# Pacing partition moves, reordering the first slab of two matmul groups, and giving the last sigmoids their own buffer

## The chip, the cores and the metric

The kernel runs on one core of a Trainium2 chip. The metric is the device time of one execution in microseconds (us). The kernel before takes 1146.32 us (median of 3 runs, 1145.93 to 1146.48). Engines: PE is TensorE, ACT is ScalarE, DVE is VectorE, SP issues most DMAs.

## The reference, cut to what matters

One decoder layer on 256 tokens with 2048 channels, all in float32. Only the last parts are touched:

```
y = rms(h);  h = h + (silu(y @ w_gate) * (y @ w_up)) @ w_down      # D_FF = 5632 = 11 * 512
y = rms(h);  h = h + sigmoid(y @ w_ple_gate) * (p @ w_ple_proj)
out = rms(h) * final_norm_g
```

Before them stand an input projection, four mixers and an output projection.

## The kernel before, in words

**Layout.** The residual is held channel-major: 16 tiles of 128 channels (partitions) by 256 tokens. Every float32 operand of a product is split into a high part that TensorE reads in its fast 32-bit format (F32R) and a low part (the rest); a product is high x high, high x low and low x high.

**Slabs.** Weights stream in slabs of 512 rows by 512 columns (1 MB). `load_slab` (L236) issues the DMA into one of 3 `raw` buffers; ACT then writes `whi` (a copy, 128x2048) and DVE writes `wlo` = raw - whi. There are 3 `whi` and 3 `wlo` buffers, so the split of a slab waits until PE has finished the slab three before it. `run` (L411) keeps two slabs loaded ahead of the one that is multiplied; after each slab's matmuls it calls `pump(budget)` (L300), which runs deferred work by cost until a credit is used up. The order in which the code emits work is close to the order on each engine, but the framework may put a ready instruction ahead of one that still waits. Each engine runs its own list in order.

**The gated feed-forward part.** `ffn` (L789) is called four times, with 3, 3, 3 and 2 column groups of 512 (`FFN_CUTS`, L29): the gate and the up product of each group, and then four `w_down` groups over all that the call has made. A group is 4 slabs (16 for the whole of D). There are two forms:

- all groups of a call but the last (7 in all) are token-major (`group_t`, L772): the activations are the stationary operand and the result is 128 tokens by 512 channels, in one PSUM bank for each half of the tokens. `ev_gate_t` and `ev_up_t` finish them; the product must then be turned to channel-major. DVE transposes it in blocks of 32x32 into a tile `turned`, and `move` (L838) carries the blocks to their partitions: 4 ACT copies of 32 partitions by 256 for each quarter i of each half t, so 8 moves and 32 copies a group. They are deferred at a cost of 1.0 each, with a budget of 2.0 a slab (`BUDGET_FFN`) and an overdraft of 2.0: 4 moves behind the group's last slab, 2 behind each of the next two.
- the last group of a call (4 in all) is channel-major (`group`, L326, `wide_out`): 4 outputs m of 128 channels, each in a PSUM bank of its own, [whi x hi + ..., wlo x hi] side by side. `ev_gate` and `ev_up` read each bank twice, ACT first and DVE after it, and no turning is needed. The first slab goes through all four outputs with whi and then through all four with wlo.

There are 6 PSUM banks for all of these products, in rotation. A channel-major group takes 4, so outputs 2 and 3 of the up group write the banks from which outputs 0 and 1 of the gate group before it are read out.

**The end.** The last 512 columns of `w_ple_gate` are done token-major: token half 0 in `last_a` (L1010), half 1 in `last_b` (L1023) in two column halves q. `gate_last` (L971) makes z = sigmoid(bank) on ACT, multiplies and adds on DVE, sums squares on ACT; `finish` (L987) makes the reciprocal root, scales, stores, and returns `rest`, which multiplies the other 12 channel tiles by a row of PSUM (5 DVE operations `h<-h,ps_bc`) and stores them. The z of half t lies in `g_row[1 + t]`.

**The pool `asp`.** It has 7 buffers (tag "a") of 8 KB a partition. At the end it holds 4 tiles of the normed residual, 2 tiles `kept` with the split of the last product's first slab (read by both token halves) and the row tile `g_row`. `load_g` (L921) evaluates `asp.tile(...)` inside a generator, so that it asks for four tiles, not for four parts of one.

Of the kernel before, what the change touches and what calls it, by code (L numbers as in the profile page):

```python
# [9 lines left out]
F32 = mybir.dt.float32  # L10
# [5 lines left out]
P = 128  # L16
# [3 lines left out]
KD = D // P  # L20
GW = 512
# [10 lines left out]
CONV_DVE = 8  # L32
BUDGET = 2.8
BUDGET_OUT = 2.8
BUDGET_FFN = 2.0
OVERDRAFT = 2.0
WARM = 9

# [14 lines left out]
def trunk(ctx: ExitStack, tc: tile.TileContext, xT, pT, par, w_in, sgu_wT, sgu_lb, sgu_b,  # L53
# [5 lines left out]
    asp = ctx.enter_context(tc.tile_pool(name="asp", bufs=7))  # L59
# [7 lines left out]
    def act(out, in_, func=AF.Copy, bias=0.0, scale=1.0):  # L67
        nc.scalar.activation(out, in_, func, bias=bias, scale=scale)  # L68

    def tt(out, a, b, op):  # L70
        nc.vector.tensor_tensor(out=out, in0=a, in1=b, op=op)  # L71
# [7 lines left out]
    def short():  # L79
        return work.tile([P, T], F32, tag="short", name="short", bufs=9)  # L80

    def duo(pad=PADP):

        return work.tile([P, 2, PADP + T], F32, tag="duo", name="duo", bufs=5)[:, :, PADP - pad:]
# [12 lines left out]
    def bank():  # L97
        return mm.tile([P, 512], F32, tag="mm", name="ps_mm")

    def wk(tag, n=T, bufs=2):  # L100
        return work.tile([P, n], F32, tag=tag, name=tag, bufs=bufs)
# [130 lines left out]
    steps = []  # L232
    now, credit = [0], [0]
    bg, fill = [], deque()
# [61 lines left out]
    def defer(cost, fn, wait=0):  # L296

        bg.append((now[0] + wait, cost, fn))

    def pump(n):  # L300

        credit[0] += n
        while credit[0] > -OVERDRAFT:
            i = next((i for i, x in enumerate(bg) if x[0] <= now[0]), None)
            if i is not None:
                _, cost, fn = bg.pop(i)
            elif fill and credit[0] > 0:
                cost, fn = fill.popleft()
            else:
                credit[0] = min(credit[0], 0.0)  # L310
                return
            fn()
            credit[0] -= cost
# [5 lines left out]
    def flush():  # L319

        while bg or fill:
            now[0] += 0 if any(x[0] <= now[0] for x in bg) else 1
            pump(1e9)
        credit[0] = 0
# [77 lines left out]
    def token_products(ps, t, tiles, parts, start, stop, x=slice(0, 512)):  # L402

        c = slice(t * P, (t + 1) * P)
        for j, (a, (whi, wlo)) in enumerate(zip(tiles, parts)):
            nc.tensor.matmul(ps, a[:, 0, c], whi[:, x], start=start and j == 0, stop=False)  # L406
            nc.tensor.matmul(ps, a[:, 0, c], wlo[:, x], start=False, stop=False)  # L407
            nc.tensor.matmul(ps, a[:, 1, c], whi[:, x], start=False,  # L408
                             stop=stop and j == len(tiles) - 1)
# [13 lines left out]
    full = [(i, 4) for i in range(0, KD, 4)]  # L423
# [284 lines left out]
    def project(cols, evac, **kw):  # L708
# [4 lines left out]
            hooks={1: [stats_first], 2: [rest_first]})  # L713
# [55 lines left out]
    hs2, h2_parts = [None] * KD, Quads()  # L769
    acc3 = wk("acc", bufs=2)  # L770

    def group_t(w, g, evac, hooks=None):  # L772

        ps = []

        def body(i, parts):
            if i == 0:
                ps.extend(bank() for _ in range(TT))
            for t in range(TT):
                token_products(ps[t], t, hs[4 * i:4 * i + 4], parts, i == 0, i == 3)  # L780
                if i == 3:
                    evac(t, ps[t])
            for f in (hooks or {}).get(i, ()):
                f()

        for i in range(KD // 4):
            steps.append(((w, 4 * i, 4, [(g * GW, GW)]), lambda p, i=i: body(i, p), BUDGET_FFN))

    def ffn(g0, ng, final):  # L789
        acts = Quads()  # L790
        gs = {}

        def ev_gate(m, ps):
            l = short()
            act(l, ps[:, T:])
            z = short()
            tt(z, ps[:, :T], l, ALU.add)
            tt(z, z, stats["ffn"][1], ALU.mult)
            s = short()
            act(s, z, AF.Sigmoid)  # L800
            tt(s, s, stats["ffn"][1], ALU.mult)
            gs[m] = short()
            tt(gs[m], z, s, ALU.mult)

        def ev_up(m, ps):
            l = short()
            act(l, ps[:, T:])
            o = short()
            tt(o, ps[:, :T], l, ALU.add)
            tt(o, o, gs[m], ALU.mult)  # L810
            split(o, acts[4 * (ng - 1) + m])

        def ev_gate_t(t, ps):
            r = stats["ffn"][0][:, t:t + 1]
            s = wide()
            act(s, ps, AF.Sigmoid, scale=r)
            gs[t] = wide()
            stt(gs[t], ps, r, s, ALU.mult, ALU.mult)  # L820

        def ev_up_t(n):
            turned = []

            def f(t, ps):
                if not turned:
                    turned.append(asp.tile([P, TT, 2, GW], F32, tag="a", name="turned"))
                o, hi = gs[t], wide()
                stt(o, ps, stats["ffn"][0][:, t:t + 1], o, ALU.mult, ALU.mult)
                act(hi.bitcast(F32R), o)  # L830
                tt(o, o, hi, ALU.subtract)
                nc.vector.transpose(out=turned[0][:, t, 0, :], in_=hi)
                nc.vector.transpose(out=turned[0][:, t, 1, :], in_=o)
                for i in range(4):
                    defer(1.0, lambda i=i: move(n, t, i, turned[0]))
            return f

        def move(n, t, i, turned):  # L838
            acts[4 * n]
            c = slice(t * P + 32 * i, t * P + 32 * i + 32)  # L840
            for j in range(4):
                act(acts.q[n][32 * j:32 * j + 32, :, :, c].rearrange("p m s b -> p s m b"),
                    turned[32 * i:32 * i + 32, t].rearrange(
                        "p s (m j b) -> p s m j b", m=4, j=4)[:, :, :, j, :])

        def hidden(i):
            if bg:
                flush()
            return [acts[k] for k in range(4 * i, 4 * i + 4)]

        h4s = lambda i: hs[4 * i:4 * i + 4]
        for n, g in enumerate(range(g0, g0 + ng)):
            hooks = ({i + 1: [f] for i, f in enumerate(stats_hooks(acc2, "ffn"))}
                     if g == 0 else None)
            if n < ng - 1:
                group_t(w_gate, g, ev_gate_t, hooks)
                group_t(w_up, g, ev_up_t(n))
            else:
                group(w_gate, [(g * GW, GW)], full, h4s, ev_gate, BUDGET_FFN, wide_out=True)
                group(w_up, [(g * GW, GW)], full, h4s, ev_up, BUDGET_FFN, wide_out=True)  # L860
        for g in range(4):
            def ev(m, ps, g=g):
                j = 4 * g + m
                add_residual(j, ps)
                if final:
                    hs2[j] = split(h[j], h2_parts[j], col("g_ple", j))
                    square(j, acc3)
            group(w_down, [(g * GW, GW)], [(4 * g0 + k, 4) for k in range(0, 4 * ng, 4)],
                  hidden, ev, wide_out=True,
                  hooks={0: [(lambda: load_p()) if g == 2 else (lambda: p_tiles(0))]}  # L870
                  if final and g > 1 else None)
# [40 lines left out]
    for g in range(3):  # L912
        group(w_pp, [(g * GW, GW)], [(0, 2)], p_tiles, evac_p(g),
              hooks={0: [ple_stats[0]]} if g == 2 else None)
# [4 lines left out]
    h_last, base, g_row = [None] * TT, [], []  # L919

    def load_g():  # L921
        g_row.extend(asp.tile([P, 4, GW], F32, tag="a", name="g_row")[:, i] for i in range(4))
        nc.sync.dma_start(out=g_row[0], in_=g_last.broadcast_to([P, GW]))

    def turn(t):
# [22 lines left out]
    for g in range(3):  # L948
        def ev(m, ps, g=g):
# [7 lines left out]
            if m == 3:  # L957
                gated()

        hooks = {0: [ple_stats[1], load_g], 1: [lambda: turn(0)], 2: [lambda: turn(1)]}  # L960
        group(w_pg, [(g * GW, GW)], full, lambda i: hs2[4 * i:4 * i + 4], ev, wide_out=True,
              hooks=hooks if g == 0 else None)
# [6 lines left out]
    z_last, zg_last, part = [None] * TT, [None] * TT, [None] * TT  # L969

    def gate_last(t, q, ps):  # L971

        if q == 0:
            z_last[t] = g_row[1 + t].rearrange("p (a t) -> p a t", a=2)
            zg_last[t] = wide()
            part[t] = wk("part", 2)
        z, x = z_last[t][:, q, :], slice(q * T, (q + 1) * T)
        act(z, ps, AF.Sigmoid, scale=stats["ple"][0][:, t:t + 1])
        tt(z, z, pp_last[t][:, x], ALU.mult)
        tt(z, z, h_last[t][:, x], ALU.add)  # L980
        nc.scalar.activation(short(), z, AF.Square, scale=D ** -0.5,
                             accum_out=part[t][:, q:q + 1])
        tt(zg_last[t][:, x], z, g_row[0][:, x], ALU.mult)
        if q == 0:
            ts(part[t][:, 0:1], part[t][:, 0:1], base[0][:, t:t + 1], ALU.add, -0.5, ALU.mult)
# [97 lines left out]
```

## Time and profile before

| what | value |
|---|---|
| median of the runs | 1146.32 us |
| the profiled execution | 1146.52 us |
| its span, first to last instruction | 1144.8 us |
| PE / PEld / DVE / ACT busy | 98 / 85 / 67 / 57 % |
| chain that ended last | PE 85 %, ACT 6 %, DVE 5 %, issue 3 %, DMA 1 % |
| mean share of the 16 DMA engines in use by the weight queue | 55.3 % |
| granted TensorE clock, mean | 0.996 |

In a timeline a row is a run of equal instructions: start, time from the first start to the last end, engine, line, operation, what it writes and reads, count, and in brackets the idle time of the engine before it with what ended it. Matmuls are pipelined: one lasts longer in the rows than the step from its start to the next.

### The profile page before, as it was taken

To read this page: it belongs to the slowest core of one execution; us is meant where nothing else is said; L and a number is where in the kernel's file an instruction comes from. 1 tells how busy PE (TensorE), PEld (TensorE's weight loads), DVE (VectorE), ACT (ScalarE), POOL (GpSimd) and SP (SyncE) were. 2 spreads that over 40 slices of the span, in tenths; PEclk is the share of its full clock that TensorE was granted. 3 is DMA by queue.
4 is the path that set the end of the run, shared out by engine and by line. 5 is a ranking of instruction groups with operands and counts; after the bars stand their busy time and mean duration, and the time that the engine had idled before them with its cause. 6 is when DMAs were issued, how large, how long until landed. Compare 5 with 4: busy or idle time off the path is not lost.

```text
span 1144.8 us, 15164 instructions
## 1 busy us (share of the span) xinstructions
PE 1116.4 (98%) x6048; PEld 967.5 (85%) x6048; DVE 772.2 (67%) x1028; ACT 654.7 (57%) x898; POOL 2.7 (0%) x15
## 2 busy tenths in 40 slices
PE   9999999999999999999999999999999998999995
PEld 7888888889887888888778888878788887889885
DVE  7789998979745575554557555555755555886784
ACT  8677687647565843346675333568533456656562
POOL 0000000000000000000000000000000000000000
PEclk9999999999999999999999999999999999999998
DMA  9855555554646555555645565554656555546632
GB/s 310 273 193 185 184 184 174 194 185 157 220 149 221 171 195 185 184 188 180 217 139 199 198 202 185 180 191 145 221 184 204 174 176 182 187 154 227 210 116 74
DMA packets 117286, 214.48 MB, mean 187 GB/s; under 512 B 4320, under 2 KB 19552, under 8 KB 117216
## 3 DMA queue, kind: packets, MB, share of 16 engines
q1 hardware_dynamic: 114640, 212.20, 55.3%
q10 hardware_dynamic: 2576, 1.32, 0.4%
q8 instruction: 47, 0.77, 0.3%
q14 instruction: 23, 0.19, 0.0%
HBM read 211.41 MB, written 2.10 MB: 187 GB/s over the span
## 4 chain that ended last, share of the span: by engine, by line
PE 85%; ACT 6%; DVE 5%; issue 3%; DMA 1%; ACTq 0%; DVEq 0%
PE ps_mm L348 56%; PE ps_mm L407 9%; PE ps_mm L408 9%; PE ps_mm L406 8%; ACT a L68 3%; ACT whi L68 2%; DVE wlo L71 2%; PE ps_mm L351 2%; PE ps_mm L353 1%; DMA wide<-sgu_lb 1%; DMA h<-xT 0%; DVE cv L71 0%; DVE short L71 0%; DVE h L71 0%; ACT duo L68 0%
## 5 line engine op out<-in xcount | busy, mean ns | idle before, releaser
L71 DVE TENSOR_TENSOR wlo<-raw,whi 128x2048 fp32r<-128x2048 f32 (+2 forms) x205 | 451.6, 2206 | 317.0 <-ACT whi L68 314.1
L68 ACT ACTIVATE whi<-raw 128x2048 fp32r<-128x2048 f32 (+2 forms) x205 | 377.9, 1847 | 305.1 <-PE ps_mm L348 136.1
L348 PE MATMUL ps_mm<-a,whi 128*128 128x512 f32 x2048 | 485.7, 391 | 9.8 <-DVE short L71 9.6
L348 PEld LDWEIGHTS ps_mm<-a,whi 128*128 128x128 f32 x2048 | 378.3, 188 | 87.3 <-DVE short L71 12.1
L348 PEld LDWEIGHTS ps_mm<-a,wlo 128*128 128x128 f32 x2048 | 257.6, 191 | 9.7 <-DVE wlo L71 3.0
L348 PE MATMUL ps_mm<-a,wlo 128*128 128x256 f32 x2048 | 261.5, 283 | 2.2 <-DVE wlo L71 2.2
L407 PE MATMUL ps_mm<-wlo,a 128*128 128x512 f32 (+1 forms) x520 | 200.0, 385 | 2.1 <-DVE wlo L71 2.0
L406 PE MATMUL ps_mm<-whi,a 128*128 128x512 f32 (+1 forms) x520 | 199.8, 386 | 0.7 <-ACT a L68 0.7
L408 PE MATMUL ps_mm<-whi,a 128*128 128x512 f32 (+1 forms) x520 | 199.6, 384 | 0.0
L407 PEld LDWEIGHTS ps_mm<-wlo,a 128*128 128x128 f32 x520 | 97.6, 188 | 23.1 <-DVE wlo L71 4.2
L406 PEld LDWEIGHTS ps_mm<-whi,a 128*128 128x128 f32 x520 | 97.7, 188 | 20.7 <-ACT a L68 1.6
L408 PEld LDWEIGHTS ps_mm<-whi,a 128*128 128x128 f32 x520 | 97.7, 188 | 19.6 <-DVE a L77 0.2
L68 ACT ACTIVATE a<-turned 32x256 fp32r<-32x256 f32 x224 | 93.1, 415 | 3.4
L71 DVE TENSOR_TENSOR h<-ps_mm,h 128x256 f32<-128x256 f32 (+1 forms) x168 | 61.7, 430 | 3.4 <-PE ps_mm L348 3.0
L68 ACT ACTIVATE duo<-long_duo,prm 128x256 f32<-128x256 f32 x108 | 45.4, 499 | 1.5 <-DVE duo L71 1.1
L71 DVE TENSOR_TENSOR cv<-cv,duo 128x512 f32<-128x512 f32 x54 | 37.0, 690 | 3.7 <-ACT duo L68 0.7
L68 ACT ACTIVATE short<-short 128x256 f32<-128x256 f32 x28 | 11.6, 414 | 42.0 <-DVE short L71 41.9
L68 ACT ACTIVATE short<-ps_mm 128x256 f32<-128x256 f32 x44 | 16.4, 372 | 22.4 <-PE ps_mm L348 22.0
L68 ACT ACTIVATE a<-h,prm 128x256 fp32r<-128x256 f32 x32 | 16.0, 501 | 19.4 <-DVE h L71 19.1
L77 DVE SCALAR_TENSOR_TENSOR wide<-ps_mm,rsy,wide 128x512 f32<-128x512 f32 x28 | 20.7, 747 | 9.0 <-ACT wide L68 5.3
L68 ACT ACTIVATE wide<-wide 128x512 fp32r<-128x512 f32 (+1 forms) x20 | 12.4, 622 | 21.4 <-DVE wide L77 21.1
L71 DVE TENSOR_TENSOR short<-short,r 128x256 f32<-128x256 f32 x44 | 18.6, 423 | 6.7 <-ACT short L68 6.0
(139 smaller groups left out, 479.2 us busy)
## 6 DMA issues: line engine op xcount, KB each, us to landing
raw<-w_gate SPq DMA_DIRECT2D x44, 1024.0 KB, 5.0
raw<-w_up SPq DMA_DIRECT2D x44, 1024.0 KB, 5.0
raw<-w_down SPq DMA_DIRECT2D x44, 1024.0 KB, 5.1
raw<-w_in SPq DMA_DIRECT2D x20, 1024.0 KB, 5.1
raw<-w_out SPq DMA_DIRECT2D x16, 1024.0 KB, 5.0
raw<-w_pg SPq DMA_DIRECT2D x16, 1024.0 KB, 5.1
raw<-w_in SPq DMA_DIRECT2D x36, 256.0 KB, 5.5
raw<-w_in SPq DMA_DIRECT2D x6, 512.0 KB, 6.8
```

The costliest lines, as they stand in the source:

```text
L68: nc.scalar.activation(out, in_, func, bias=bias, scale=scale)
L71: nc.vector.tensor_tensor(out=out, in0=a, in1=b, op=op)
L77: nc.vector.scalar_tensor_tensor(out=out, in0=a, scalar=s, in1=b, op0=op0, op1=op1)
L348: nc.tensor.matmul(o, w, r, start=first, stop=final)
L351: nc.tensor.matmul(o, w, a[:, 0, :], start=first, stop=final and low == 1)
L353: nc.tensor.matmul(o, w, a[:, 1, :], start=False, stop=final)
L406: nc.tensor.matmul(ps, a[:, 0, c], whi[:, x], start=start and j == 0, stop=False)
L407: nc.tensor.matmul(ps, a[:, 0, c], wlo[:, x], start=False, stop=False)
L408: nc.tensor.matmul(ps, a[:, 1, c], whi[:, x], start=False, stop=stop and j == len(tiles) - 1)
```

## The change

- The moves go into a queue of their own, `moves`. Behind each slab of a feed-forward group one move (one quarter of one token half) is taken from it, first behind the last slab of the group that made it. The budget of these slabs is 0. What is left before `w_down` is done there.
- The channel-major gate and up groups get `halves=True`: in the first slab the first two outputs go through whi and wlo of all four row blocks, and then the other two.
- `load_g` asks for one tile; z of the last sigmoids lies in a tile of the pool "duo" (5 buffers).

```diff
-BUDGET_FFN = 2.0
...
+    moves = deque()
+
+    def one_move():
+        if moves:
+            moves.popleft()()
...  in group_t's body, behind the slab's products, evacuation and hooks
+            one_move()
-            steps.append(((w, 4 * i, 4, [(g * GW, GW)]), lambda p, i=i: body(i, p), BUDGET_FFN))
+            steps.append(((w, 4 * i, 4, [(g * GW, GW)]), lambda p, i=i: body(i, p), 0.0))
...  in ev_up_t
-                    defer(1.0, lambda i=i: move(n, t, i, turned[0]))
+                    moves.append(lambda i=i: move(n, t, i, turned[0]))
...
         def hidden(i):
-            if bg:
-                flush()
+            while moves:
+                one_move()
...
-                group(w_gate, [(g * GW, GW)], full, h4s, ev_gate, BUDGET_FFN, wide_out=True)
-                group(w_up, [(g * GW, GW)], full, h4s, ev_up, BUDGET_FFN, wide_out=True)
+                for w, ev in ((w_gate, ev_gate), (w_up, ev_up)):
+                    group(w, [(g * GW, GW)], full, h4s, ev, wide_out=True, halves=True,
+                          hooks={i: [one_move] for i in range(KD // 4)})
...
     def load_g():
-        g_row.extend(asp.tile([P, 4, GW], F32, tag="a", name="g_row")[:, i] for i in range(4))
+        g_row.append(asp.tile([P, 4, GW], F32, tag="a", name="g_row")[:, 0])
...
-            z_last[t] = g_row[1 + t].rearrange("p (a t) -> p a t", a=2)
+            z_last[t] = duo(0)
```

The order that `halves` gives the first slab is already in `group` (L361):

```
            if halves and i == 0 and not last:
                todo = [(m, j, low) for ms_ in (order[:2], order[2:]) for low in (0, 1)
                        for j in range(nk) for m in ms_]
```

## Rows read from the trace of the kernel before

**Rows 1.** The page's first part: busy time, share of the span, instructions

```profile
PE 1116.4 (98%) x6048; PEld 967.5 (85%) x6048; DVE 772.2 (67%) x1028; ACT 654.7 (57%) x898; POOL 2.7 (0%) x15
```

**Rows 2.** Waits of PE, 300 to 970 us: total us, times, longest

```profile
PE ps_mm L348 <- DVE short L71: 9.6, 8, 1.6
PE ps_mm L348 <- DVE wlo L71: 2.2, 4, 0.6
PE ps_mm L407 <- DVE wlo L71: 2.0, 3, 0.7
```

**Rows 3.** Timeline of PE, first feed-forward call, its channel-major gate and up groups

```profile
379.22 7.44 PE L348 MATMUL ps_mm<-a,whi 128*128 128x512 f32 x32
...
389.13 2.17 PE L348 MATMUL ps_mm<-a,wlo 128*128 128x256 f32 x16 [0.56 <-DVE wlo L71]
...
397.02 2.57 PE L348 MATMUL ps_mm<-a,whi 128*128 128x512 f32 x10 [1.61 <-DVE short L71]
...
402.40 1.19 PE L348 MATMUL ps_mm<-a,whi 128*128 128x512 f32 x4 [0.78 <-DVE short L71]
```

**Rows 4.** Timeline of PE, same call, last slab of its second token-major gate group

```profile
343.57 0.39 PE L406 MATMUL ps_mm<-whi,a 128*128 128x512 f32 x1
344.63 0.50 PE L407 MATMUL ps_mm<-wlo,a 128*128 128x512 f32 x1 [0.67 <-DVE wlo L71]
344.97 0.40 PE L408 MATMUL ps_mm<-whi,a 128*128 128x512 f32 x1
```

**Rows 5.** Timeline of ACT behind the first token-major up group

```profile
327.50 1.92 ACT L68 ACTIVATE whi<-raw 128x2048 fp32r<-128x2048 f32 x1
...
330.05 10.26 ACT L68 ACTIVATE a<-turned 32x256 fp32r<-32x256 f32 x24
340.34 1.92 ACT L68 ACTIVATE whi<-raw 128x2048 fp32r<-128x2048 f32 x1
342.28 3.39 ACT L68 ACTIVATE a<-turned 32x256 fp32r<-32x256 f32 x8
```

**Rows 6.** Timeline of DVE, the same stretch: last transpose, next split

```profile
331.21 0.67 DVE L833 STREAM_TRANSPOSE turned<-wide 128x512 f32<-128x512 f32 x1
...
342.29 2.29 DVE L71 TENSOR_TENSOR wlo<-raw,whi 128x2048 fp32r<-128x2048 f32 x1 [8.23 <-ACT whi L68]
```

**Rows 7.** Timeline of ACT, end of the channel-major gate group

```profile
390.19 3.72 ACT L68 ACTIVATE whi<-raw 128x2048 fp32r<-128x2048 f32 x2
```

**Rows 8.** Timeline of DVE, end of that gate group and end of the up group

```profile
392.14 4.49 DVE L71 TENSOR_TENSOR wlo<-raw,whi 128x2048 fp32r<-128x2048 f32 x2 [3.06 <-ACT whi L68]
396.55 0.42 DVE L71 TENSOR_TENSOR short<-ps_mm,short 128x256 f32<-128x256 f32 x1
...
401.93 0.42 DVE L71 TENSOR_TENSOR short<-ps_mm,short 128x256 f32<-128x256 f32 x1
...
417.94 0.42 DVE L71 TENSOR_TENSOR short<-ps_mm,short 128x256 f32<-128x256 f32 x1 [0.18 <-ACT short L68]
```

**Rows 9.** Timeline of PE, the last 25 us

```profile
1119.60 0.50 PE L204 MATMUL ps_sum<-ones,acc 128*128 128x1 f32 x4
...
1126.41 0.28 PE L408 MATMUL ps_mm<-a 128*128 128x256 f32 x1
...
1131.45 0.28 PE L408 MATMUL ps_mm<-whi,a 128*128 128x256 f32 x1
1132.29 0.49 PE L1001 MATMUL ps_bc<-dg_last,ones 128*128 128x128 f32 x2 [0.57 <-DVE dg_last L74]
```

**Rows 10.** Timeline of ACT, the last 25 us

```profile
1126.73 1.20 ACT L68 ACTIVATE g_row<-ps_mm,rsy 128x256 f32<-128x256 f32 x3 [8.63 <-PE ps_mm L408]
...
1132.76 0.45 ACT L68 ACTIVATE g_row<-ps_mm,rsy 128x256 f32<-128x256 f32 x1
```

**Rows 11.** Timeline of DVE, the last 25 us

```profile
1132.82 2.01 DVE L71 TENSOR_TENSOR h<-h,ps_bc 128x256 f32<-128x256 f32 x5 [0.58 <-PE ps_bc L1001]
1134.75 0.88 DVE L71 TENSOR_TENSOR g_row<-g_row,wide 128x256 f32<-128x256 f32 x2
```

## Prediction, made before the changed kernel was run

> **What bounds the kernel now.** Start with the page's busy times: PE is busy for 1116.4 us, 98 % of the span [rows 1]. No other engine comes near, so a change that adds and removes no matmul can win only where PE stands still or slows. The second view is the list of PE's waits over the feed-forward part, 300 to 970 us [rows 2]: 15 waits of three kinds, 13.8 us together. The reader should see that they repeat: 8 = 2 in each of the four calls, 4 = 1 in each, 3 = 1 in each of the calls that have two token-major groups. One call therefore shows all of them, and the timelines of the first are the third view.
>
> What a wait costs is more than its idle time, since rows show pipelined matmuls. A 512-column matmul stands for 0.39 us but starts every (7.44 - 0.39)/31 = 0.227 us [rows 3, 4], so an idle time of 0.67 is a step of 1.06 (343.57 to 344.63), 0.83 longer than usual: idle plus 0.16. For 256 columns it is the same, 0.28 [rows 9] less (2.17 - 0.28)/15 = 0.13 [rows 3], some 0.15. The step behind a wait is slow as well, 0.34 instead of 0.227 (344.63 to 344.97) [rows 4], 0.11 more.
>
> Why PE waits there: ACT carries 24 move copies in 10.26 us (0.427 each) in front of the split at 340.34 [rows 5], and DVE has to wait 8.23 us for that split before it can make `wlo` [rows 6]; PE wants it at 343.8 and has it at 344.6 [rows 4]. In the channel-major gate group the same lag shows three times: `wlo` late by 0.56, then outputs 2 and 3 of the up group late by 1.61 and 0.78 [rows 3]. These last two wait for the gate group's banks. DVE reads the first of them only at 396.55, behind two splits in a row, 392.14 to 396.6 [rows 8], which are late because ACT makes their `whi` only at 390.19 to 393.9 [rows 7].
>
> The end is the fourth view. Token half 0 is complete in PSUM at about 1119.6, when the sums behind it start [rows 9], yet ACT makes its first sigmoid at 1126.73, after 8.63 idle us [rows 10]. The row names PE, but no product of half 0 ends there; what ends at 1126.41 + 0.28 is half 1's second use of the `kept` tile [rows 9]. The code says why: four tiles of normed residual, two of `kept` and the row tile fill the pool's 7 buffers, so the z tiles wait for `kept`. All of half 0's work then falls on the last matmuls and behind them.
>
> **The change part by part.** Sums go against the profiled execution, 1146.52 us (span 1144.8 and 1.7 around it); the median is 0.2 lower.
>
> *Pacing the moves.* No instruction is added or removed: 7 groups x 32 copies = 224 remain. Behind the up group's last slab the split of the next gate group's last slab has 2 moves in front of it instead of 4 + 2: 8 copies, 3.4 us. From 330.05 that is 333.5. Its buffer is free when the slab three back is done, 2 slabs of 24 x 0.227 = 5.45 us before 343.57, so 332.7. Split (1.92) and `wlo` (2.29) [rows 5, 6] then end near 337.8, and PE wants it at 343.8: 6 us to spare where 0.8 are missing. Each later slab has ACT work of 1.92 + 4 x 0.427 = 3.6 us in 5.45, so no lag builds up. The three 0.67 and the four 0.56 waits go: 3 x (0.67 + 0.16 + 0.11) + 4 x (0.56 + 0.15 + 0.11) = 2.8 + 3.3 = 6.1 us. Bounds: 6.1 and, on the other side, the loss that the last rival prices. I take all of it, nearest to the row of the unburdened split at 327.50 [rows 5], a whole slab ahead of its use.
>
> *First two outputs first.* With no lag, DVE reads the gate group's bank 0 soon after its last matmul: for the up group, where ACT carries no moves, the first read comes at 417.94 with 0.18 us of idle time before it [rows 8], and the `w_down` group behind, with the same four of six banks and not reordered, appears in no wait [rows 2]. The reorder gives more: output 2 starts behind 8 + 8 matmuls, 8 x (0.227 + 0.13) = 2.9 us into the slab instead of 0.45. Either alone could cover the 1.61; the 0.78 behind it needs the lag gone. `wlo` of that slab is wanted 1.8 us earlier; the 6 us to spare hide it, and without that cover it would cost up to 1.8 in each of 8 groups. Gain 4 x (1.61 + 0.78 + 2 x 0.16 + 2 x 0.11) = 11.7 us. Bounds: 11.7 and that loss, -14. In the gate group's last slab DVE has a split and four evacuations of four 0.42 us operations, 9 us in the 16 x (0.227 + 0.13) = 5.7 of a slab, so I set 0.9 of both parts together aside for short new waits.
>
> A rule speaks against this part. The waits have the look of one kind: PE held at the same place in every call, by a bank that is not yet free [rows 2, 3]. The Trainium skill (Perfetto Trace Analysis, Optimization Strategy) says that the same gap repeating on the engine that should be saturated can mean that there is not enough PSUM or SBUF for the next tile, that is, too few buffers. By that the 11.7 us stay, since the six banks stay; by the rows they go. It is a rival below.
>
> *Own buffer for z.* It takes nothing from the FFN part. Half 0's sigmoids can start at about 1119.9. From the first sigmoid to `dg_last` it took 1126.73 to 1132.29 [rows 9, 10], 5.5 us, so `rest` of half 0 (matmuls 0.49, 5 DVE operations in 2.01) [rows 9, 11] falls at about 1125.5 to 1128, under half 1's matmuls. At the end half 1's last sigmoid starts 0.3 behind 1131.45 instead of at 1132.76, and its first DVE operation 0.5 later, at 1132.3 instead of 1134.75, where it stands behind the five operations of half 0 [rows 11]: 2.5 us. The rest's matmuls now stand in PE's stream, 0.4. Net 2.1. Bounds: 2.5, and 0 if the order on DVE stays; a loss only if the rest's matmul stands in PE's stream ahead of its input at 1125.5, and the first column half ends five steps of 0.13 ahead of 1126.41 [rows 9], at 1125.8. The new pool has 5 buffers and its other users are through, so no wait is added there.
>
> Sum: 6.1 + 11.7 - 0.9 + 2.1 = 19.0. 1146.5 - 19.0 = 1127.5.
>
> **The rivals.**
>
> *Banks are the limit.* Moves and z act as above, the bank waits stay: 11.7 - 0.9 = 10.8 more, 1138.3. For it: the waiting tile is a bank in 8 of 15 waits. Against it: the unreordered `w_down` groups on the same banks.
>
> *Half of it.* The lag shrinks but output 3 of the up group still waits as it does now, 4 x (0.78 + 0.27) = 4.2, and the tail keeps its order, 2.1: 1133.8. For it: output 1 of the gate group was read 5.4 us behind output 0 (396.55 and 401.93 [rows 8]) with a split between, an order that could stay.
>
> *The change doesn't do what it says.* A move needs nothing of PE, so where ACT idles its place in the code need not hold; the splits stay late and only the end gains: 1144.4.
>
> *The bunch grows, slower.* The same mechanism further: with no budget to hold them, all 8 moves run ahead of the waiting split at 340.34. Spare there is below zero today, so each move beyond the 6 in front of it (24 copies) costs PE 4 x 0.427 = 1.7 us in each of 7 groups; two more are 3.4 x 7 = 24, less 10.8 of bank waits and 2.1 of the end: 1157.4. It decides from 29 copies in front on, 5 x 0.427 x 7 = 14.9 against 12.9. For it: the split at 327.50 ran ahead of moves that the code has before it, so code order isn't fixed. Against it: the 8 moves at 342.28 had their input by 331.9 and still stayed behind the split that the code has before them [rows 5, 6]; six of the eight stand behind it now.
>
> **How the numbers follow.** Forecast 0.66, half 0.15, banks 0.09, not done 0.05, bunched 0.04, other 0.01. The likeliest gives 1127.5, less 0.2 for the median: 1127.3. The range reaches down to the full bounds, 6.1 + 11.7 + 2.5 = 20.3, or 1126, and a little for waits that I don't see: 1125.5. Upward it takes in the half case and stops short of the banks: 1136. What can be told from no change is about 0.2 %, 2.3 us. Faster by more: forecast, half and banks, 0.90; same, with the not-done case, 0.06; slower 0.04.
>
> **What would show it.** Right: PE's list of waits between 300 and 970 us is empty or under 2 us; on ACT the copies stand in fours with a split between; DVE's waits of 8.2 us for `whi` are gone; the sigmoids of half 0 start near 1120 and the five operations of its rest end before the last matmul. Wrong step by step: 24 copies in a row still (pacing); waits of the up group's third output with `wlo` in time (banks); the first sigmoid still behind a matmul on `kept` (buffer). The whole is wrong if PE shows new waits for `whi` or for turned tiles in `w_down`.

## The result, and the profile after

The changed kernel takes 1127.38 us (median of 4 runs, 1126.62 to 1127.98) against 1146.12: a ratio of 0.9837, 95 % interval 0.982 to 0.9854. A second set of runs gave 1127.34 and 0.9835 (0.9822 to 0.9849). The profiled execution took 1127.98 us with a span of 1126.2, 18.6 less than before.

The page's first part, as in [rows 1]: the span, then busy time, share and instructions. Each engine has as many instructions as before. PE has lost 3 us of busy time. Most of it can be laid to the slow steps at the waits, as an estimate: by the prediction's working 0.16 + 0.11 us each, 4.1 for 15, of which some 1.5 are left. Its share of the span has risen because most of its idle time has gone.

```profile
span 1126.2 us, 15154 instructions
PE 1113.4 (99%) x6048; PEld 967.3 (86%) x6048; DVE 772.2 (69%) x1028; ACT 655.9 (58%) x898; POOL 2.2 (0%) x15
```

The list of PE's waits between 300 and 970 us, three kinds and 13.8 us before [rows 2], is empty. PE's timeline at the same place as [rows 3]:

```profile
389.75 5.63 PE L347 MATMUL ps_mm<-a,whi 128*128 128x512 f32 x24
395.22 1.11 PE L347 MATMUL ps_mm<-a,wlo 128*128 128x256 f32 x8
396.17 2.35 PE L347 MATMUL ps_mm<-a,whi 128*128 128x512 f32 x8
398.36 3.02 PE L347 MATMUL ps_mm<-a,wlo 128*128 128x256 f32 x24
```

No row has an idle time in brackets. One is a little long: eight products at 396.17 should last 7 x 0.227 + 0.39 = 1.98 us and last 2.35. That 0.37 is what is left of the bank waits, once in each of the four calls (the same eight products last 2.34 to 2.36 in the others). DVE, the counterpart of [rows 8], shows why:

```profile
391.79 2.29 DVE L70 TENSOR_TENSOR wlo<-raw,whi 128x2048 fp32r<-128x2048 f32 x1 [2.22 <-PE ps_mm L347]
394.00 0.42 DVE L70 TENSOR_TENSOR short<-ps_mm,short 128x256 f32<-128x256 f32 x1
...
396.16 0.42 DVE L70 TENSOR_TENSOR short<-ps_mm,short 128x256 f32<-128x256 f32 x1
```

The first bank is free at 394.4 and wanted at 396.2; the second is free at 396.6, wanted one product later, at 396.4. ACT, the counterpart of [rows 5] and [rows 7], in the stretch that leads there:

```profile
373.95 3.41 ACT L67 ACTIVATE a<-turned 32x256 fp32r<-32x256 f32 x8
377.39 1.92 ACT L67 ACTIVATE whi<-raw 128x2048 fp32r<-128x2048 f32 x1
379.33 5.97 ACT L67 ACTIVATE a<-turned 32x256 fp32r<-32x256 f32 x14
385.33 1.92 ACT L67 ACTIVATE whi<-raw 128x2048 fp32r<-128x2048 f32 x1
387.27 2.54 ACT L67 ACTIVATE a<-turned 32x256 fp32r<-32x256 f32 x6
389.84 1.92 ACT L67 ACTIVATE whi<-raw 128x2048 fp32r<-128x2048 f32 x1
391.78 1.70 ACT L67 ACTIVATE a<-turned 32x256 fp32r<-32x256 f32 x4
393.50 0.39 ACT L67 ACTIVATE short<-ps_mm 128x256 f32<-128x256 f32 x1
```

Here the copies don't stand in fours, as the code has them: there are 8, 14, 6 and 4 of them, without a gap between them and the splits, until the first read of a bank at 393.50. ACT still has a backlog, but no run of copies in this kernel is longer than 14, where 24 stood before.

The end, ACT and then DVE, is to be held against [rows 10] and [rows 11]. Half 0's last product starts at 1103.1 and its sums at 1103.3; its sigmoids follow at 1103.5, 0.2 us behind the sums. Before, they came seven us behind them. The five operations of its rest (four rows of `h<-h,ps_bc`, the last with two) lie between 1109.94 and 1113.08, ahead of the last product at 1115.38, and half 1's last sigmoid is not held up.

```profile
1103.52 0.84 ACT L67 ACTIVATE duo<-ps_mm,rsy 128x256 f32<-128x256 f32 x2 [1.70 <-PE ps_mm L407]
...
1115.69 0.47 ACT L67 ACTIVATE duo<-ps_mm,rsy 128x256 f32<-128x256 f32 x1 [3.79 <-PE ps_mm L407]
```

```profile
1109.94 0.42 DVE L70 TENSOR_TENSOR h<-h,ps_bc 128x256 f32<-128x256 f32 x1 [1.73 <-PE ps_bc L1009]
...
1112.34 0.74 DVE L70 TENSOR_TENSOR h<-h,ps_bc 128x256 f32<-128x256 f32 x2
1116.20 0.89 DVE L70 TENSOR_TENSOR duo<-duo,wide 128x256 f32<-128x256 f32 x2 [3.12 <-ACT duo L67]
```

From the start of the last product to the end of the span it was 13.3 us (1131.45 to 1144.8) and is 10.9 (1115.38 to 1126.2). From the start of half 0's sums, 1119.6 and 1103.3, it was 25.2 and is 22.9: 2.3 less, with the rest's products counted in.

### The profile page after: what moved, and what is told of

The parts are those of the page before. It is cut to its first block, busy times and chain, and to the rows that moved or that the text cites. A ratio compares the mean times of both kernels' runs of the same rounds, so it can differ in the third digit from the quotient of the medians.

```text
span 1126.2 us, 15154 instructions
## 1 busy us (share of the span) xinstructions
PE 1113.4 (99%) x6048; PEld 967.3 (86%) x6048; DVE 772.2 (69%) x1028; ACT 655.9 (58%) x898; POOL 2.2 (0%) x15
## 4 chain that ended last, share of the span: by engine, by line
PE 90%; DVE 5%; DMA 3%; ACT 1%; issue 1%; SPq 1%; ACTq 0%; DVEq 0%
PE ps_mm L347 57%; PE ps_mm L405 10%; PE ps_mm L406 10%; PE ps_mm L407 10%; DVE wlo L70 2%; PE ps_mm L350 2%; DMA h<-xT 2%; PE ps_mm L352 1%; DVE short L70 1%; ACT whi L67 1%; DMA raw<-w_in 0%; DMA wide<-sgu_lb 0%; DVE duo L70 0%; DVE cv L70 0%; SPq L249 0%
## 5 line engine op out<-in xcount | busy, mean ns | idle before, releaser
L70 DVE TENSOR_TENSOR short<-ps_mm,short 128x256 f32<-128x256 f32 x44 | 18.5, 419 | 7.1 <-ACT short L67 6.7
```

## The experiments

Times are medians; the kernel before ran beside each at 1146.2 to 1146.3.

**One edit at a time.**

*z_only*: the kernel before with the third edit alone.

```diff
-        g_row.extend(asp.tile([P, 4, GW], F32, tag="a", name="g_row")[:, i] for i in range(4))
+        g_row.append(asp.tile([P, 4, GW], F32, tag="a", name="g_row")[:, 0])
-            z_last[t] = g_row[1 + t].rearrange("p (a t) -> p a t", a=2)
+            z_last[t] = duo(0)
```

> The kernel before with the third edit alone: z in a tile of the pool duo, one row tile. Theory (the z tiles wait for a slot that kept gives back): token half 0's sigmoids start right behind its last product, the five operations of its rest run under half 1's matmuls, and the span loses 2.1 us (0 to 2.5): near 1144.0. The feed-forward waits stay at 13.8 us. Rival (the order on DVE stays, only the place of z changes): 1146.1.

Measured: 1143.64 us, 0.9977 (0.9968 to 0.9986), 2.6 less, with an interval of 1.6 to 3.7. Half 0's sigmoids start at 1119.77, and the feed-forward waits stay (13.9 us).

*z_slice*: the kernel before, one tile of `asp` for the row and both z.

```diff
-        g_row.extend(asp.tile([P, 4, GW], F32, tag="a", name="g_row")[:, i] for i in range(4))
+        row = asp.tile([P, 4, GW], F32, tag="a", name="g_row")
+        g_row.extend(row[:, i] for i in range(4))
```

> The kernel before with load_g asking for one tile of the pool asp and taking four slices of it, so that z lies in the row's own tile and no pool changes. Slot theory (z waited for a seventh-plus-one buffer): one tile fits beside the six, the sigmoids start behind half 0's last product, 1143.6 as with z in duo. Rival (z must be apart from the row tile, which other operations read): no gain, 1146.2.

Measured: 1143.45 us, 0.9979 (0.997 to 0.9989). The pool "duo" is not what helps; asking for four tiles where one fits was the fault.

*p_only*: the changed kernel without `halves` and with z as before, that is, the pacing alone.

> The changed kernel without its second and third edits: moves one a slab, six banks, first slab in the old order. Lag theory: the seven waits for wlo go (6.1 us) and with them most of the waits for the banks (up to 11.7 us): 1129 to 1134, the latter if output 3 still waits 0.78 in each call. Bank theory (six banks are too few): only the 6.1 us go, the waits of 1.61 and 0.78 stay: 1140.

Measured: 1139.75 us, 0.9946 (0.9931 to 0.9961). Of PE's waits in the feed-forward part those for `wlo` are gone, and those for the banks are nearly what they were (9.6 us before):

```profile
PE ps_mm L347 <- DVE short L70: 8.6, 8, 1.7
```

DVE's timeline of this kernel, and then PE's, to be held against those of the changed kernel above:

```profile
391.59 2.29 DVE L70 TENSOR_TENSOR wlo<-raw,whi 128x2048 fp32r<-128x2048 f32 x1 [2.22 <-ACT whi L67]
393.80 0.42 DVE L70 TENSOR_TENSOR short<-ps_mm,short 128x256 f32<-128x256 f32 x1
...
395.96 0.42 DVE L70 TENSOR_TENSOR short<-ps_mm,short 128x256 f32<-128x256 f32 x1
```

```profile
389.51 4.27 PE L347 MATMUL ps_mm<-a,whi 128*128 128x512 f32 x18
394.27 0.51 PE L347 MATMUL ps_mm<-a,whi 128*128 128x512 f32 x1 [0.49 <-DVE short L70]
396.44 3.24 PE L347 MATMUL ps_mm<-a,whi 128*128 128x512 f32 x13 [1.66 <-DVE short L70]
```

DVE reads the two banks 0.2 us earlier here than in the changed kernel. What differs is when PE wants them: behind two products of the up group (393.6 and 394.5), where `halves` wants them at 396.2 and 396.4. The time is the one that the bank theory gave; whether the banks are too few or read too late this run alone doesn't say.

*h_only*: the kernel before with `halves=True` in the two calls of `group`, the bursts as they were.

> The kernel before with the second edit alone: halves in the channel-major gate and up groups, moves in bursts as before. Lag theory: the seven waits for wlo stay (6.1 us); output 2 is wanted 2.4 us later and no longer waits 1.61, but output 3 waits for a bank that DVE reads at the same late time, so that of 11.7 us between 0 and 7.5 go: near 1141. Rival (the order of the first slab is what held PE): all 11.7 go, 1134.4.

Measured: 1151.07 us, 1.0042 (1.0027 to 1.0057): slower, which neither theory had. PE's waits in the whole span:

```profile
PE ps_mm L348 <- DVE short L71: 10.8, 4, 2.7
...
PE ps_mm L348 <- DVE wlo L71: 2.1, 4, 0.5
PE ps_mm L407 <- DVE wlo L71: 2.0, 3, 0.7
```

The two bank waits of a call have become one, a little longer than both together (2.7 us against 1.61 + 0.78): DVE reads the second bank at 401.90, as in [rows 8], and PE goes on at 402.37, where before it went on at 402.40, with as much work left. So far nothing is lost. The loss comes behind it. PE's timeline there, and then stretches of the same run (us, PE, PEld, DVE, ACT, POOL busy, granted clock, DMA share, GB/s):

```profile
402.37 2.07 PE L348 MATMUL ps_mm<-a,whi 128*128 128x512 f32 x4 [2.69 <-DVE short L71]
```

```profile
380.00:399.00 19.00, 18.47 (x103) 15.99 (x102) 8.40 (x7) 15.43 (x26) 0.00 (x0) 1.00 0.51 166
402.00:408.00 6.00, 5.63 (x21) 5.14 (x22) 3.12 (x5) 2.60 (x3) 0.00 (x0) 0.50 0.55 179
...
608.50:612.00 3.50, 3.50 (x24) 3.18 (x23) 1.53 (x4) 2.61 (x3) 0.00 (x0) 1.00 0.79 280
811.50:814.50 3.00, 3.00 (x12) 2.61 (x12) 0.91 (x3) 1.74 (x2) 0.00 (x0) 0.50 0.81 259
972.00:975.00 3.00, 3.00 (x14) 2.81 (x14) 1.08 (x3) 2.19 (x3) 0.00 (x0) 0.50 0.90 319
```

PE ran at the full clock, stood still for 2.7 us, and came back at 0.50, the lower of its two levels (1.2 of 2.4 GHz). Behind the same wait of the other calls it was 1.00, 0.50 and 0.50 (the last three rows). The next wait for `wlo` then comes at 550.4 instead of at 547.6. Over the span the mean clock is 0.991 instead of 0.996 (1150.6 and 1144.8 us): 0.009 and 0.004 of the span, 10.4 and 4.6 us, are lost, 5.8 more than before, and the span is 5.8 longer. The kernel before, whose longest single wait there is 1.61 us, keeps 1.00 through the feed-forward part.

**What a copy in front of a split costs.** *bunch*: the kernel before with one constant changed.

```diff
-BUDGET_FFN = 2.0
+BUDGET_FFN = 8.0
```

> The kernel before with the budget of a feed-forward slab at 8.0 instead of 2.0: all 8 moves behind the up group's last slab. Theory (a split waits for the moves in front of it, 0.427 us a copy): 32 copies in front instead of 24, the split 3.4 us later at each of 7 places without spare: +24 us, 1170, with wlo waits of some 4 us each. Rival (the order of the code does not hold on ACT, the split takes its place among the moves as soon as its buffer is free): no more than 2 us either way, 1144 to 1148.

Measured: 1169.79 us, 1.0208 (1.0191 to 1.0225). The time is that of the theory, but not for its reason alone. ACT has 32 copies in a row, the split comes at 343.56 instead of 340.34, and PE waits for `whi` itself: 13.7 + 8.6 = 22.3 us of idle time where the kernel before has 13.8.

```profile
PE ps_mm L348 <- ACT whi L68: 13.7, 4, 3.4
PE ps_mm L406 <- ACT whi L68: 8.6, 6, 2.0
```

That is 8.5 more. The rest is the clock again, a mean of 0.982 over 1167.5 us: 21.0 - 4.6 = 16.4 us. The sum, 24.9, is near the 22.7 by which the span grew. The clock fell not only behind the waits of 3.4 us, but also behind two shorter ones close to each other, neither as long as h_only's 2.7 us. PE's timeline, and then the stretch behind:

```profile
345.52 0.73 PE L406 MATMUL ps_mm<-whi,a 128*128 128x512 f32 x2 [1.97 <-ACT whi L68]
347.32 0.72 PE L406 MATMUL ps_mm<-whi,a 128*128 128x512 f32 x1 [1.07 <-ACT whi L68]
```

```profile
347.50:350.50 3.00, 3.00 (x7) 2.19 (x8) 3.00 (x3) 1.57 (x1) 0.00 (x0) 0.50 0.45 110
```

My 24 left the clock out and counted the bank waits as if they stayed; they are no longer in the list (PE's own waits for `whi` probably give DVE the time to read the banks). The time fits by two errors that cancel: luck.

**Late readers or too few banks.** *p_pool*: as p_only, with the copies on GpSimd; banks and order of the products as in the kernel before.

```diff
-                act(acts.q[n][32 * j:32 * j + 32, :, :, c].rearrange("p m s b -> p s m b"),
-                    turned[...])
+                nc.gpsimd.tensor_copy(out=acts.q[n][...], in_=turned[...])
```

> Pacing alone (no halves, z as before) with the moves' copies on GpSimd instead of ACT, so that ACT has only splits and evacuations. Lag theory (the banks are late because ACT carries moves in front of the splits and the first reads): the waits of output 2 and 3, 2.2 us idle a call, vanish on the same six banks and in the same order, 1139.75 less 11.7: 1128. Bank theory (six banks are too few for this order): they stay, 1140. If GpSimd's copies are too slow for w_down, PE shows waits for turned tiles there instead.

Measured: 1129.25 us, 0.9854 (0.984 to 0.9869). No wait of PE in the feed-forward part is left. DVE reads the two banks 3.5 and 3.3 us sooner than in p_only:

```profile
390.25 0.43 DVE L70 TENSOR_TENSOR short<-ps_mm,short 128x256 f32<-128x256 f32 x1 [0.86 <-ACT short L67]
...
392.67 0.41 DVE L70 TENSOR_TENSOR short<-ps_mm,short 128x256 f32<-128x256 f32 x1
```

Six banks in the old order are enough, but for some 0.3 us a call (see *What is left*), once ACT has no copies in front of its reads. The rule of the Trainium skill weighed in the prediction (Perfetto Trace Analysis, Optimization Strategy) names too few buffers as one possible cause of such repeating gaps. Here it was another: a backlog on ACT, which takes the first read of each bank and makes the `whi` that DVE needs before it gets to its own.

**The clock.** *h_fill*: h_only with ten products that nobody reads put between the two halves of the up group's first slab.

```diff
+                if filler is not None and n_done == len(todo) // 2:
+                    for _ in range(10):
+                        nc.tensor.matmul(filler, parts[0][0][:, :P],
+                                         tiles[0].rearrange("p a t -> p (a t)"), start=True, stop=True)
```

> The second edit alone (bursts as before) with ten idle 128x512 products, 2.27 us, between the two halves of the up group's first slab, where PE waits 2.7 us in each call; their result is read by nobody. Clock theory (after that wait the granted clock is 0.50 for 13.65 us in all, which costs half of it, 6.8): the idle time falls to 0.4 us a call, the clock stays at 1.00, and the time falls although work was added: 1151.1 - 6.8 = 1144.3. Rival (the halved order itself is slower): 1151 or more.

Measured: 1154.52 us, 1.0079 (1.0062 to 1.0096). A miss in time: the ten products took the place of all but one of the 4 + 9 useful ones that h_only does ahead of its wait, so the wait only shrank to 2.15 us. The added 2.27 us a call, 9.1 in all, were paid, less 2.2 of idle time and, by the mean clocks of 0.995 and 0.991, some 4.6 of lost cycles: 2.3 by this sum, 1.7 by the spans (1150.6 and 1152.3). But in the profiled execution the clock stayed up in the same stretch:

```profile
402.00:408.00 6.00, 5.12 (x34) 4.71 (x35) 4.04 (x8) 3.18 (x5) 0.00 (x0) 1.00 0.57 186
```

It was 1.00 behind the waits of the other three calls as well. So the halved order does not lower the clock by itself: in these two profiles it fell behind three of four waits of 2.7 us and behind none of those of 2.15. The other three executions of h_fill had mean clocks of 0.992 to 0.994, where the profiled one had 0.995, so in them the clock may have fallen somewhere. The Trainium skill (TensorE: Matmul & The Clock Gate, HAM oscillation — how this bites in real kernels) tells of a matmul kernel that is throttled again behind each of its waits for data. These traces agree in part: the clock did not fall behind every wait, and in the feed-forward part of the kernel before, with waits of up to 1.61 us, behind none.

**What is left.** *a_half* and, in a later set of runs, *a_half2*: the changed kernel with the copies of odd j on DVE.

```diff
...  in place of the call of act
+                if j % 2:
+                    nc.vector.tensor_copy(out=o, in_=x)
+                else:
+                    act(o, x)
```

> The changed kernel with half of each move's copies (j odd) on DVE. Lag theory: ACT's backlog at the gate group's end is 8 copies shorter, the last four waits of PE (0.07 idle, 0.35 with the slow step behind) go: 1127.4 - 1.4 = 1126.0. Rival (DVE, which reads the banks and makes wlo, becomes the late one): waits grow, 1128 to 1132.

> The changed kernel with the copies of odd j on DVE, on the same chip: 1126.0, 1.4 below the changed kernel.

Measured: 1125.98 us, 0.9825 (0.981 to 0.984), and 1126.11, 0.9826 (0.9812 to 0.9839). In a_half2 ACT is through with the copies before the gate group's last slab, and idle ahead of the first read:

```profile
378.38 3.83 ACT L67 ACTIVATE a<-turned 32x256 fp32r<-32x256 f32 x9
382.24 1.92 ACT L67 ACTIVATE whi<-raw 128x2048 fp32r<-128x2048 f32 x1
385.63 1.92 ACT L67 ACTIVATE whi<-raw 128x2048 fp32r<-128x2048 f32 x1 [1.47 <-PE ps_mm L347]
390.35 0.39 ACT L67 ACTIVATE short<-ps_mm 128x256 f32<-128x256 f32 x1 [2.80 <-PE ps_mm L347]
```

*a_pool*, *pz_pool* and *after_again*, in one set with a_half2: the changed kernel with the copies on GpSimd, with `halves` and without, and the changed kernel as it is.

> The changed kernel, all three edits, with the moves on GpSimd. The four waits of 0.07 that the change leaves go: 1126.0, as with half of the copies on DVE, and within 1 us of the same kernel without halves. Rival (GpSimd's copies are late for w_down or slow DVE): 1127.4 or more.

> Moves on GpSimd one a slab, z in duo, the first slab in the old order: the changed kernel without halves, and with ACT free of moves. If the reorder only covers ACT's backlog, it is not needed here: 1129.25 - 2.6 = 1126.7. Rival (the reorder has a worth of its own): slower than the same kernel with halves by over 1 us.

> The changed kernel as it is, on the same chip as the two with GpSimd: 1127.4.

Measured: a_pool 1125.92 (0.9823, 0.9809 to 0.9836), pz_pool 1127.22 (0.9835, 0.9821 to 0.9848), after_again 1127.34. The three versions with the reorder and without the backlog stand 1.2 to 1.4 us below the changed kernel. The intervals of their ratios overlap with that of the changed kernel, so the medians alone don't show that they beat it. The profiles do, read by stage: from the start of the first token-major product of the feed-forward part to the start of the sums behind that part, PE takes

| kernel | from | to | us |
|---|---|---|---|
| before | 282.93 | 1037.48 | 754.55 |
| p_only | 283.07 | 1030.49 | 747.42 |
| changed kernel | 283.31 | 1021.36 | 738.05 |
| after_again | 282.46 | 1020.55 | 738.09 |
| p_pool | 282.29 | 1019.94 | 737.65 |
| pz_pool | 282.32 | 1019.95 | 737.63 |
| a_pool | 282.32 | 1019.00 | 736.68 |
| a_half | 283.16 | 1019.83 | 736.67 |
| a_half2 | 282.80 | 1019.44 | 736.64 |

Two executions of one kernel agree here within 0.05 us. The backlog that the change leaves costs 1.4 us, which are the four slow steps: the eight products of 2.35 us last 2.00 in a_half2.

```profile
395.64 2.00 PE L347 MATMUL ps_mm<-a,whi 128*128 128x512 f32 x8
```

And the reorder is worth about 1 us even without a backlog, as the rival to pz_pool's expectation had it (the medians of pz_pool and a_pool are 1.3 apart). Neither has a wait in the list, but pz_pool's first slab of the up group has 32 products in 7.68 us where 32 usually take 7.44 [rows 3], and 7.73 in the other three calls:

```profile
388.76 7.68 PE L347 MATMUL ps_mm<-a,whi 128*128 128x512 f32 x32
```

## Why the prediction was right, and where a step of it was not

The forecast was 1127.3 and the time is 1127.38. That it fits to 0.1 us is luck. The feed-forward part was to gain 6.1 + 11.7 - 0.9 = 16.9 us and gained 16.5 (754.55 to 738.05); the end was to gain 2.1 and gained 2.3. The prices of the waits were right: all of them together, 17.8, are nearly what a_half2 gains there, 17.9. That is why the time came out although the picture of how the waits would go was wrong in part. Of the signs, the list of waits is empty, DVE's waits of 8.2 us for `whi` are gone (the longest is 5.6), and half 0's sigmoids and rest came as forecast; the copies in fours did not come. As the list is empty, the rivals *Half of it* and *The change doesn't do what it says* fell. By its steps:

- *Pacing the moves* was put at 6.1 us and gave 6.45 alone by the medians. The seven waits for `wlo` went, and those for the banks, which the step doesn't count, shrank by 1.0. But the step's picture failed: "Each later slab has ACT work of 1.92 + 4 x 0.427 = 3.6 us in 5.45, so no lag builds up". ACT took the copies ahead of the code's order, in runs of 10, 11 and 11 behind one group and 8, 14, 6 and 4 behind the next; that a copy needs nothing of PE is the likely reason. The edit cut the runs from 24 to at most 14, and behind 14 the split still met its time.
- *First two outputs first* was put at 11.7 less 0.9 and gives 9.4 on top of the pacing in the feed-forward part (747.42 to 738.05). Of the 1.4 less, 1.0 is what the pacing had already taken from the bank waits. The rest is the 0.9 set aside for short new waits, mis-sized: the slow steps that are left take 1.4. The reason was half right. "With no lag, DVE reads the gate group's bank 0 soon": the lag stayed. "Either alone could cover the 1.61": pacing alone covers neither wait (p_only), and halves alone makes one wait of the two and lowers the clock behind it (h_only, 4.9 slower). While ACT carries the copies, the bank waits go only with both edits: pacing brings the reads to 394.0 and 396.2, halves moves PE's want to 396.2 and 396.4. Alone the two change the time by -6.45 and +4.9, together by some -16.3 (1146.2 - 1127.34, less the 2.56 of z_only; no run has just these two).
- *Own buffer for z* was put at 2.5 less 0.4, 2.1 net, and gave 2.56 alone, of which the interval can't tell 2.1 from 2.5. The traces can: behind the last product 2.5 are won, as forecast, and 2.3 from half 0's sums on. The mis-sized term is the price of the rest's products in PE's stream. PE's timeline of the changed kernel there:

```profile
1109.40 0.28 PE L407 MATMUL ps_mm<-whi,a 128*128 128x256 f32 x1
1109.52 0.38 PE L1009 MATMUL ps_bc<-dg_last,ones 128*128 128x128 f32 x2
1109.66 0.36 PE L405 MATMUL ps_mm<-a 128*128 128x256 f32 x1
1109.86 0.28 PE L406 MATMUL ps_mm<-a 128*128 128x256 f32 x1
```

From 1109.40 to 1109.86 are two usual steps of 0.12 and 0.22 more, not 0.4.
- *Banks are the limit* fell in p_pool. For pacing alone its time, 1140, was right, but by another cause: the banks were read late.
- *The bunch grows* was the right mechanism for what copies in front of a split do (bunch), with the wrong accounts: the clock was the larger part. It did not come about, as the runs of copies became shorter. Its argument has a misreading: the row at 342.28 [rows 5] is 8 copies, that is, 2 moves, not 8 moves.

## What to carry to other kernels

A wait of the busiest engine on a buffer has two sides: when the reader lets go and when the writer wants it. Look at both times before counting a gain, since an edit on one side may be worth nothing, or less, until the other is done. Work that depends on nothing late need not keep its place in the code: look in the trace for how long a run of it the engine really makes, or give it to an engine that has room. And compare two versions by the length of the stage that was changed: here it told 1 us apart where the medians of four or five runs, with their intervals, could not.

## What the runs showed of the hardware

- A single wait of TensorE of 2.7 us in the middle of full work was followed by a granted clock of 0.50 in three calls of four (h_only), and so was a pair of waits of 1.97 and 1.07 us with 0.73 us of work between them (bunch). With about as much idle time as before (14.9 us of listed waits against 13.8), h_only lost 5.8 us to it.
- GpSimd's copy of 32 partitions by 256 between partition groups takes 0.395 us (median of 224, p_pool), ACT's 0.415 (before), DVE's 0.286 (a_half).
- While GpSimd copies, DVE's operations are longer. In p_pool the product of two 128x256 tiles `short<-short,r` has a median of 0.60 us in the 16 cases that overlap a copy, and 0.42 in the 28 others. The rows are the view of the tile `turned`, one of the 16 in DVE's timeline, and the copies under it in GpSimd's (POOL):

```profile
L849 POOL CAST a<-turned x224: 390/395/2481, 329.5 to 949.3; 32x256 fp32r<-32x256 f32 x112
```

```profile
393.12 0.60 DVE L70 TENSOR_TENSOR short<-short,r 128x256 f32<-128x256 f32 x1
```

```profile
391.98 2.00 POOL L849 CAST a<-turned 32x256 fp32r<-32x256 f32 x4
```
